# Moving the token-layout load of x, its norm and the first evacuation three weight chunks later in a hybrid decoder trunk

## The chip, the cores and the metric

The kernel runs on 1 core of one Trainium2 chip. The metric is the device time of one launch in microseconds (us), taken as the median of several runs.

## The reference, cut to what matters

One decoder layer on 256 tokens with 2048 features, all in f32. What the change touches is the very first step: the input is normalised by an RMS norm and multiplied by one wide projection.

```python
def rms_norm(x, g):
    xf = x.astype(jnp.float32)
    y = xf * lax.rsqrt(jnp.mean(xf * xf, axis=-1, keepdims=True) + EPS)
    return (y * g.astype(jnp.float32)).astype(x.dtype)
...
        h = rms_norm(x, g_mix[i])
        z = h @ w_in[i]
        (sc_b, sc_c, sc_x, cf_a, cf_g, q, k, v, g_out, gk_lr,
         m_a, m_b, m_c) = jnp.split(z, split_points, axis=-1)
```

Three token mixers (short convolution, Conformer convolution, gated linear attention), a merge, a SwiGLU FFN, a per-layer-embedding step and a final norm follow.

## The kernel before

**Products.** Every large product keeps the activations stationary (feature by token, 128x128 blocks) and streams weights of up to 512 columns. f32 accuracy comes from splitting both sides into a high and a low part and adding three matmuls: high by high (L244), high by the weight's low part (L245), low by the weight's high part (L246), all in `products`. A weight is split by `split` (L109): ScalarE writes `whi` (L110), VectorE writes `wlo` (L111).

**Groups and chunks.** A `Group` is one block of output columns; its 2048 input features are taken in four chunks of four 128-row tiles. A chunk is 24 matmuls (4 tiles, 2 halves of the tokens, 3 products). Chunks are numbered through the whole plan: the group `k` 0 is chunks 0 to 3, `k` 1 is 4 to 7, `gk` is 8 to 11, then `q`, `v` and so on.

**The loop.** `run` (L250) goes through the chunks. In iteration i it issues the transfers of chunk i+2 (`issue`, on the SP queue), splits chunk i+1 (`split_w`), runs what has been put off to this iteration (`deferred`), scales the activations that chunk i needs (`g.pre`, for the first group only), writes the matmuls, and after a group's last chunk calls its `evac`. This fixes the order in the source. The order on each engine's instruction stream can differ from it, which the rows of the engines' timelines show.

**The start.** The RMS norm is not applied to the input ahead of the first product. Its gain is: `h_pre` (L351) scales x by features (tiles `x`, 512 KB a chunk, transferred at L164 and L173) by `g_mix` and splits it into `hhi` (ScalarE, L321) and `hlo` (VectorE, L322 through the helper at L104). The root of the mean square is a factor per token, so it is applied when a group leaves PSUM. For that factor x is loaded a second time, by tokens: two tiles `xt` of 128x2048 (1024 KB each, L176). `x_norm` (L359) squares each on ScalarE with a running sum (L363) and makes the reciprocal root `rt` from the sums (a ScalarE square root at L301 and small VectorE operations).

**Where these steps stand.** `xt` is issued after the weights of chunks 3 and 4. `x_norm` is called by `ev_k0`, the evacuation of chunk 3. `ev_k0` puts the rest off to iteration 5: `load_consts` (SP transfers of `gnb` and two `lm` mask tiles, VectorE casts) and the evacuation proper, which copies the two accumulators, scaled by `rt`, into `fk` (ScalarE, L407) and puts their transposes off by two more iterations.

**Buffers.** `raws` and `wparts` have 5 buffers each, and a chunk takes two of them. The PSUM pool `acc` has 5 banks, and a group takes two. `xt` takes two of the 13 large tiles.

Of the kernel before, what the change touches and what calls it, by code (L numbers as in the profile page):

```python
# [28 lines left out]
LAG = 2  # L29
# [34 lines left out]
def kernel(  # L64
# [5 lines left out]
    nc = tc.nc  # L70
# [13 lines left out]
    def nm(s):  # L84
        uid[0] += 1
        return f"{s}_{uid[0]}"

    def big(name, shape=(P, 8, T), dt=F32):
        return t8.tile(list(shape), dt, tag="t8", name=nm(name))

    def med(name, shape=(P, 2, NB), dt=F32):
        return t4.tile(list(shape), dt, tag="t4", name=nm(name))
# [4 lines left out]
    def sm(name, n, tag):  # L97
        return small.tile([P, n], F32, tag=tag, name=nm(name))
# [50 lines left out]
    x_v = x[0].rearrange("(h p) d -> p h d", p=P)  # L149
# [3 lines left out]
    chunks = []  # L153
    state = {"dma": 0, "split": 0}

    def issue(c):
        g = c.g
        c.raw = []
        for k in c.ks[::2]:
            r = raws.tile([P, 2, g.n], F32, tag="raw", name=nm("raw"))  # L160
            if c is chunks[0]:

                for q in range(2):
                    nc.sync.dma_start(out=xs[0][:, k + q, :], in_=x_feat[:, k + q, :])  # L164
                    nc.sync.dma_start(out=r[:, q, :], in_=g.w[:, k + q, g.c0 : g.c0 + g.n])
            else:
                nc.sync.dma_start(out=r, in_=g.w[:, k : k + 2, g.c0 : g.c0 + g.n])
            c.raw.append(r)
        if c in chunks[:3]:
            z = chunks.index(c) + 1  # L170
            if z == 2:
                nc.sync.dma_start(out=vec[:, 16:], in_=vecs[:, 16:])
            nc.sync.dma_start(out=xs[z], in_=x_feat[:, 4 * z : 4 * z + 4, :])  # L173
        if c in chunks[3:5]:
            xt = big("xt", (P, D))
            nc.sync.dma_start(out=xt, in_=x_v[:, chunks.index(c) - 3, :])  # L176
            x_tok.append(xt)

    def split_w(c):
# [17 lines left out]
    deferred = []  # L197
# [3 lines left out]
    def defer(i, fn):  # L201
        deferred.append((i + LAG, fn))
# [47 lines left out]
    def run(plan):  # L250
# [3 lines left out]
        while now[0] < len(chunks):  # L254
            i = now[0]
            c = chunks[i]
            while state["dma"] < min(len(chunks), i + PREF_DMA + 1):
                issue(chunks[state["dma"]])
                state["dma"] += 1
# [37 lines left out]
    def rsqrt(ss, n, scale, tag):  # L297
        v = sm("v", n, tag + "v")
        ts(v, ss, scale, EPS, ALU.mult, ALU.add)
        s = sm("s", n, tag + "s")  # L300
        act.activation(out=s, in_=v, func=AF.Sqrt)  # L301
        y = sm("y", n, tag + "y")
        dve.reciprocal(out=y, in_=s)
        newton(y, s, v)
        return y
# [53 lines left out]
    def x_norm():  # L359

        ss = sm("sx", 2, "sx")
        for h in range(2):
            act.activation(out=x_tok[h], in_=x_tok[h], func=AF.Square, accum_out=ss[:, h : h + 1])  # L363
        rt["1"] = rsqrt(ss, 2, 1.0 / D, "rt")
        rt["q"] = sm("rq", 2, "rq")
        dve.tensor_scalar_mul(rt["q"], rt["1"], 0.0625)

    def rs(h, key="1"):
        return rt[key][:, h : h + 1]

    def load_consts():
        nc.sync.dma_start(out=gnb, in_=g_gla_norm[0].partition_broadcast(P))
        for a in range(0, 2 * NL + 1, 8):
            n = min(8, 2 * NL + 1 - a)
            lm = med("lm", (P, 8, P), I32)
            nc.sync.dma_start(out=lm[:, :n, :], in_=masks[:, a : a + n, :])
            dve.tensor_copy(lmask[:, a : a + n, :], lm[:, :n, :])
        nc.gpsimd.memset(cmask, 1.0)
        nc.gpsimd.memset(cmask.rearrange("p (c t) -> p c t", t=64)[:, :, 0:1], 0.0)
        nc.gpsimd.memset(sT, 0.0)  # L380
        dve.tensor_copy(flip, ident[:, ::-1])


    def to_feat(key, c, src):

        if c == 0:
            featT[key] = big(key + "T")

        def sink(j, b):
            act.activation(out=featT[key][:, 4 * c + j : 4 * c + j + 2, :], in_=b, func=AF.Copy)  # L390

        transpose_block(src, sink)

    def ev_k0(g, i):
        x_norm()

        def later():
            load_consts()
            ev_feat("k", 0)(g, i)

        defer(i, later)

    def ev_feat(key, c, rkey="1", then=None):
        def f(g, i):
            m = med("f" + key)
            for h in range(2):
                act.activation(out=m[:, h, :], in_=g.ps[h], func=AF.Copy, scale=rs(h, rkey))  # L407

            def later():
                to_feat(key, c, m)  # L410
                if c == 1 and then is not None:
                    then()

            defer(i, later)

        return f
# [369 lines left out]
    def Z(name, c, ev, n=NB, pre=None, kind="tok", off=0, cost=1.3):  # L786
# [4 lines left out]

    plan = [
        Z("k", 0, ev_k0, pre=h_pre),
        Z("k", 1, ev_feat("k", 1)),
        Z("gk", 0, ev_first, 264),
# [260 lines left out]
```

## Time and profile before

| | us |
|---|---|
| median of 3 runs | 1912.35 |
| lowest, highest | 1912.32, 1913.01 |
| profiled execution | 1912.33 |
| its span in the profile | 1910.6 |

The span is the time from the first to the last instruction that the profiler recorded; 1.73 us of the profiled execution lie outside it. Busy times of different engines overlap. A matmul's end is modelled, so its start times are what to compare. In a timeline row the first number is the start, the second the duration, and the brackets at the end, where there are any, hold the idle time of that engine just before and what ended it. SPq is the queue of SyncE that issues transfers; its duration is that of issuing, not of moving the data.

### The profile page before, as it was taken

Reading aid. Unit: us, or ns where it says so; the run is one execution under the profiler, and the core shown is the slowest. Engines: PE = TensorE matmul, PEld = TensorE weight load, DVE = VectorE, ACT = ScalarE, POOL = GpSimd, SP = SyncE. Lnnn points to the kernel's source line nnn. Section 1 sums busy time; section 2 is a strip of 40 time slices with the busy share of each in tenths; the row PEclk is TensorE's granted clock in tenths of the full one; section 3 lists DMA queues with packets and bytes.
Section 4 is the critical chain, followed back from the end, with each engine's and each line's share of the span. In section 5 each row is a group of like instructions: output and inputs, shape, how many; then the busy total and the mean of one; then the engine's idle time right before and its main releaser. Section 6 shows DMA issues by size and latency. Waiting matters only on the chain.

```text
span 1910.6 us, 22740 instructions
## 1 busy us (share of the span) xinstructions
PE 1887.1 (99%) x8688; PEld 1573.0 (82%) x8688; DVE 1188.8 (62%) x1409; ACT 927.3 (49%) x1067; POOL 9.1 (0%) x22
## 2 busy tenths in 40 slices
PE   7999999999999999999999999999999999999998
PEld 5888888888888888888888888888888888888887
DVE  6447777668888888655555555555555555555555
ACT  6557556554454435644445544444344444444554
POOL 0000000000000000000000000000000000000000
PEclk9999999999999999999999999999999999999999
DMA  8666655555666656676655666665566666655553
GB/s 306 204 187 187 177 177 179 174 165 166 189 186 194 193 165 209 195 232 193 213 187 184 185 191 192 189 189 190 195 192 192 195 188 189 192 186 191 180 186 122
DMA packets 190254, 363.18 MB, mean 190 GB/s; under 512 B 11600, under 2 KB 20432, under 8 KB 189760
## 3 DMA queue, kind: packets, MB, share of 16 engines
q1 hardware_dynamic: 189248, 358.12, 61.2%
q0 software_dynamic: 896, 3.61, 0.6%
q8 instruction: 68, 1.11, 0.2%
q14 instruction: 42, 0.34, 0.1%
HBM read 359.58 MB, written 2.10 MB: 189 GB/s over the span
## 4 chain that ended last, share of the span: by engine, by line
PE 98%; DMA 1%; DVE 1%; ACT 0%; SPq 0%; issue 0%; DVEq 0%
PE acc L244 32%; PE acc L246 32%; PE acc L245 31%; PE tr L313 2%; PE sc L522 1%; DMA xt<-in_x_dram 0%; DMA x<-in_x_feat_dram 0%; DVE rw L688 0%; DVE wlo L111 0%; PE ov L592 0%; PE ov L594 0%; PE ov L593 0%; ACT whi L110 0%; ACT hhi L321 0%; PE sc L549 0%
## 5 line engine op out<-in xcount | busy, mean ns | idle before, releaser
L111 DVE TENSOR_TENSOR wlo<-raw,whi 128x1024 fp32r<-128x1024 f32 (+2 forms) x678 | 813.7, 1203 | 678.0 <-ACT whi L110 677.1
L110 ACT ACTIVATE whi<-raw 128x1024 fp32r<-128x1024 f32 (+2 forms) x678 | 706.2, 1043 | 914.7 <-PE acc L246 836.5
L244 PE MATMUL acc<-whi,hhi 128*128 128x512 f32 (+1 forms) x1120 | 434.4, 388 | 12.1 <-ACT hhi L321 6.9
L245 PE MATMUL acc<-wlo,hhi 128*128 128x512 f32 (+1 forms) x1120 | 431.2, 385 | 0.4 <-DVE wlo L111 0.4
L246 PE MATMUL acc<-whi,hlo 128*128 128x512 f32 (+1 forms) x1120 | 431.3, 385 | 0.0
L244 PE MATMUL acc<-whi,xhi 128*128 128x512 f32 (+1 forms) x832 | 321.4, 386 | 0.0
L246 PE MATMUL acc<-whi,xlo 128*128 128x512 f32 (+1 forms) x832 | 320.5, 385 | 0.0
L245 PE MATMUL acc<-wlo,xhi 128*128 128x512 f32 (+1 forms) x832 | 320.2, 385 | 0.0
L244 PEld LDWEIGHTS acc<-whi,hhi 128*128 128x128 f32 x1120 | 211.5, 189 | 53.4 <-ACT hhi L321 7.3
L245 PEld LDWEIGHTS acc<-wlo,hhi 128*128 128x128 f32 x1120 | 211.7, 189 | 42.0 <-DVE wlo L111 1.2
L246 PEld LDWEIGHTS acc<-whi,hlo 128*128 128x128 f32 x1120 | 211.4, 189 | 42.0
L246 PEld LDWEIGHTS acc<-whi,xlo 128*128 128x128 f32 x832 | 156.3, 188 | 31.5
L245 PEld LDWEIGHTS acc<-wlo,xhi 128*128 128x128 f32 x832 | 156.4, 188 | 31.0
L244 PEld LDWEIGHTS acc<-whi,xhi 128*128 128x128 f32 x832 | 156.3, 188 | 30.7
L244 PE MATMUL acc<-whi,aT 128*128 128x512 f32 x352 | 137.5, 390 | 0.0
L246 PE MATMUL acc<-whi,aT 128*128 128x512 f32 x352 | 137.1, 389 | 0.0
L245 PE MATMUL acc<-wlo,aT 128*128 128x512 f32 x352 | 136.9, 389 | 0.0
L104 DVE SCALAR_TENSOR_TENSOR cv<-uT,vec,cv 128x255 f32<-128x255 f32 (+15 forms) x240 | 110.9, 467 | 4.8
L246 PEld LDWEIGHTS acc<-whi,aT 128*128 128x128 f32 x352 | 66.1, 188 | 13.9
L245 PEld LDWEIGHTS acc<-wlo,aT 128*128 128x128 f32 x352 | 66.1, 188 | 13.6
L244 PEld LDWEIGHTS acc<-whi,aT 128*128 128x128 f32 x352 | 66.1, 188 | 13.4
L244 PE MATMUL acc<-whi,mT 128*128 128x512 f32 x128 | 50.2, 392 | 0.0
(250 smaller groups left out, 1369.4 us busy)
## 6 DMA issues: line engine op xcount, KB each, us to landing
raw<-in_w_in_dram SPq DMA_DIRECT2D x262, 512.0 KB, 3.6
raw<-in_w_gate_up_dram SPq DMA_DIRECT2D x176, 512.0 KB, 3.7
raw<-in_w_down_dram SPq DMA_DIRECT2D x88, 512.0 KB, 3.6
raw<-in_w_gla_out_dram SPq DMA_DIRECT2D x32, 512.0 KB, 3.8
raw<-in_w_o_dram SPq DMA_DIRECT2D x32, 512.0 KB, 3.6
raw<-in_w_ple_gate_dram SPq DMA_DIRECT2D x24, 512.0 KB, 3.7
raw<-in_w_sc_out_dram SPq DMA_DIRECT2D x16, 512.0 KB, 4.2
raw<-in_w_cf_out_dram SPq DMA_DIRECT2D x16, 512.0 KB, 4.4
```

Of the source, the lines that this page charges most:

```text
L104: dve.scalar_tensor_tensor(out=o, in0=a, scalar=s, in1=b, op0=op0, op1=op1)
L110: a = act.activation(out=hi, in_=src, func=AF.Copy)
L111: b = dve.tensor_tensor(out=lo, in0=src, in1=hi.bitcast(F32), op=ALU.subtract)
L244: pe.matmul(o, lhsT=shi[:, hs], rhs=whi, start=st, stop=False)
L245: pe.matmul(o, lhsT=shi[:, hs], rhs=wlo, start=False, stop=False)
L246: pe.matmul(o, lhsT=slo[:, hs], rhs=whi, start=False, stop=sp)
L313: pe.transpose(b[:, q, h * P : h * P + P], src[:, h, (j + q) * P : (j + q) * P + P], ident,)
L522: pe.matmul(b[:, e, :], lhsT=K[:, dt, :], rhs=Q[:, dt, :], start=q == 0, stop=q == 1)
```

## The change

The two transfers of x by tokens are issued after the weights of chunks 5 and 6, not 3 and 4. `ev_k0` no longer calls `x_norm` at once: it puts off to iteration i + LAG + 1 = 6 the norm, the evacuation and then `load_consts`. The evacuation gets i + LAG + 1 as its iteration, so the transposes of its result go to iteration 8, not 6 (the code before put them off to 5, but in iteration 5, whose list had been taken already).

```diff
-        if c in chunks[3:5]:
+        if c in chunks[5:7]:
             xt = big("xt", (P, D))
-            nc.sync.dma_start(out=xt, in_=x_v[:, chunks.index(c) - 3, :])
+            nc.sync.dma_start(out=xt, in_=x_v[:, chunks.index(c) - 5, :])
             x_tok.append(xt)
...
     def ev_k0(g, i):
-        x_norm()
 
         def later():
+            x_norm()
+            ev_feat("k", 0)(g, i + LAG + 1)
             load_consts()
-            ev_feat("k", 0)(g, i)
-
-        defer(i, later)
+
+        deferred.append((i + LAG + 1, later))
```

## Rows read from the trace of the kernel before

**Rows 1.** The page's first lines: the span, and the busy time of the matmuls with its share of the span.

```profile
span 1910.6 us, 22740 instructions
PE 1887.1 (99%) x8688; PEld 1573.0 (82%) x8688; DVE 1188.8 (62%) x1409; ACT 927.3 (49%) x1067; POOL 9.1 (0%) x22
```

**Rows 2.** All waits of the matmuls over the whole run: who was waited for, us in total, times, longest.

```profile
PE acc L244 <- ACT hhi L321: 6.9, 1, 6.9
PE acc L244 <- ACT whi L110: 5.3, 1, 5.3
PE mu L690 <- DVE rw L688: 1.7, 1, 1.7
PE acc L245 <- DVE wlo L111: 0.4, 1, 0.4
```

**Rows 3.** The chain of work that ended last, 15 to 35 us: start, us, what.

```profile
15.15 9.32 DMA xt<-in_x_dram
24.49 1.40 ACT xt L363
...
26.49 0.41 ACT hhi L321
```

**Rows 4.** The timeline of ScalarE, 10 to 43 us. The `hhi` rows are of chunks 1, 2 and 3, the `whi` rows of chunks 1 (both halves in one row), 2, 2, 3, 3, 4, 4 in order of time.

```profile
10.79 1.71 ACT L321 ACTIVATE hhi<-x,vec 128x256 fp32r<-128x256 f32 x4 [1.39 <-DMA x<-in_x_feat_dram]
12.40 2.18 ACT L110 ACTIVATE whi<-raw 128x1024 fp32r<-128x1024 f32 x2
16.67 1.06 ACT L110 ACTIVATE whi<-raw 128x1024 fp32r<-128x1024 f32 x1 [2.08 <-DMA raw<-in_w_in_dram]
18.11 1.06 ACT L110 ACTIVATE whi<-raw 128x1024 fp32r<-128x1024 f32 x1 [0.38 <-DMA raw<-in_w_in_dram]
20.74 1.06 ACT L110 ACTIVATE whi<-raw 128x1024 fp32r<-128x1024 f32 x1 [1.57 <-DMA raw<-in_w_in_dram]
22.05 1.06 ACT L110 ACTIVATE whi<-raw 128x1024 fp32r<-128x1024 f32 x1 [0.25 <-DMA raw<-in_w_in_dram]
24.49 1.91 ACT L363 ACTIVATE xt<-xt 128x2048 f32<-128x2048 f32 x1 [1.38 <-DMA xt<-in_x_dram]
...
26.40 1.69 ACT L321 ACTIVATE hhi<-x,vec 128x256 fp32r<-128x256 f32 x4
28.00 1.04 ACT L110 ACTIVATE whi<-raw 128x1024 fp32r<-128x1024 f32 x1
28.94 1.69 ACT L321 ACTIVATE hhi<-x,vec 128x256 fp32r<-128x256 f32 x4
30.54 1.90 ACT L363 ACTIVATE xt<-xt 128x2048 f32<-128x2048 f32 x1
...
33.49 1.28 ACT L301 ACT_TABLE_LOAD   x1
...
41.33 1.25 ACT L407 ACTIVATE fk<-acc,y 128x512 f32<-128x512 f32 x2
```

**Rows 5.** The timeline of VectorE in the same stretch: the low parts of chunk 3's weights (two in one row), then those of chunk 2's activations.

```profile
21.83 2.54 DVE L111 TENSOR_TENSOR wlo<-raw,whi 128x1024 fp32r<-128x1024 f32 x2 [1.40 <-ACT whi L110]
26.92 1.69 DVE L104 SCALAR_TENSOR_TENSOR hlo<-x,vec,hhi 128x256 fp32r<-128x256 f32 x4 [2.56 <-ACT hhi L321]
```

**Rows 6.** The timeline of the matmuls: the last one of chunk 1, the first, eleventh and twelfth of chunk 2, and the first of chunk 3.

```profile
19.69 0.39 PE L246 MATMUL acc<-whi,hlo 128*128 128x512 f32 x1
26.94 0.79 PE L244 MATMUL acc<-whi,hhi 128*128 128x512 f32 x1 [6.86 <-ACT hhi L321]
...
31.38 0.52 PE L245 MATMUL acc<-wlo,hhi 128*128 128x512 f32 x1
31.73 0.39 PE L246 MATMUL acc<-whi,hlo 128*128 128x512 f32 x1
...
34.68 0.39 PE L244 MATMUL acc<-whi,hhi 128*128 128x512 f32 x1
```

**Rows 7.** Transfers. First the SP queue's timeline: the issue of the `x` tile of chunk 2 and of the first `xt`, then six weight transfers (chunks 5, 6 and 7) in one row and the first transfer of `load_consts`; then what all queues had moved from 0 to 20 us; then, of the same 20 us, the three 512 KB transfers of `x` (count, KB each, median us from issue to landing); last, the two `xt` transfers' time to landing.

```profile
7.28 0.66 SPq L173 DMA_DIRECT2D x<-in_x_feat_dram  x1
...
15.15 0.46 SPq L176 DMA_DIRECT2D xt<-in_x_dram  x1
...
20.45 17.19 SPq L167 DMA_DIRECT2D raw<-in_w_in_dram  x6
37.69 0.46 SPq L372 DMA_DIRECT2D gnb<-in_g_gla_norm_dram  x1
...
DMA packets 3359, 6.22 MB, mean 311 GB/s; under 512 B 414, under 2 KB 1054, under 8 KB 3359
...
x<-in_x_feat_dram SPq DMA_DIRECT2D x3, 512.0 KB, 8.0
...
DMA to landing us min/median/max: 9.3/9.8/10.3
```

**Rows 8.** Busy time by stretch: length, PE, PEld, DVE, ACT and POOL busy us (with the number of instructions), the granted TensorE clock (1.00 is 2.4 GHz, 0.50 is 1.2 GHz), the DMA engines' mean share and GB/s.

```profile
24.00:24.50 0.50, 0.00 (x0) 0.00 (x0) 0.36 (x1) 0.01 (x1) 0.00 (x0) 1.00 1.04 385
24.50:25.00 0.50, 0.00 (x0) 0.00 (x0) 0.00 (x0) 0.50 (x1) 0.00 (x0) 0.81 1.07 393
...
31.50:32.00 0.50, 0.50 (x4) 0.42 (x3) 0.38 (x1) 0.50 (x1) 0.06 (x1) 0.86 1.04 381
...
600.00:720.00 120.00, 120.00 (x531) 99.41 (x530) 105.43 (x173) 49.43 (x51) 0.00 (x0) 1.00 0.59 180
```

## The prediction

> **What bounds the kernel now.** I read the page first: the matmuls are busy for 1887.1 of 1910.6 us [rows 1], so only time in which TensorE waits, or runs at its lower clock, can be won. The list of its waits holds four, and one is long: 6.9 us, for `hhi` on ScalarE [rows 2]. The chain of waits shows what is behind it: for 9.32 us the transfer of the first `xt`, then the squaring, then `hhi`, then matmuls again [rows 3]. ScalarE's timeline shows why a squaring that nobody needs yet stops the products. The stream holds, in this order, both `whi` of chunk 3, the squaring of `xt`, the four `hhi` of chunk 2 [rows 4]. The squaring started at 24.49, when its transfer had landed, and `hhi` of chunk 2 behind it at 26.40. The input of that `hhi` was there long before: its transfer was issued at 7.28, and the three of that size took 8.0 us in the median, 10.0 for the longest if it was this one, so 15.3 to 17.3 us [rows 7]. So chunk 2 waits for a transfer that is not its own.
>
> What the wait costs is read from the matmuls [rows 6]. At full clock thirteen starts of chunk 2 take 34.68 - 31.73 = 2.95 us, 0.227 each. Chunk 1's last matmul started at 19.69, so chunk 2 could have started at 19.92 and started at 26.94: 7.02 us. Its first eleven starts took 31.73 - 26.94 = 4.79 us where 11 x 0.227 = 2.50 would do: 2.29 us more. The granted clock is 1.00 at 24.0 to 24.5 us, 0.81 in the next half and 0.86 at 31.5 to 32.0 [rows 8], so about from 24.8 to 31.6 it was at 1.2 GHz. The whole that can be won is 7.02 + 2.29 = 9.31 us.
>
> From 32 us on TensorE waited once more, 1.7 us for a sum of the Conformer norm [rows 2]. VectorE, which is late there, is busy for 105 of the 120 us from 600 to 720 [rows 8]; it is not full, and its weight splits follow the matmuls through the `wparts` buffers. So what is won at the start shifts all later work and comes off the end in full.
>
> **The change part by part.** *The squaring leaves its place.* Its transfer is now issued behind the weights of chunk 5. The second half of those takes the buffer that the first half of chunk 3 frees, when `wlo` is written: 21.83 + 2.54 / 2 = 23.1 us [rows 5]. A transfer of `xt` then lands 9.3 to 10.3 us later [rows 7], at 32.8 to 33.8, or sooner where less is queued. In the source the call now stands behind chunk 6's weight issue and split, three iterations later. I take it that the squaring then stands behind `hhi` of chunks 2 and 3: already before, the second `xt`, issued behind chunk 4's weights, stands behind both [rows 4].
>
> *What is late next.* The order of the rest I keep as it was: `whi`, `whi` of chunk 3, then `hhi` of chunk 2. Nothing that comes before these in a queue is changed, and before, `hhi` was placed behind both although its input had landed before chunk 2's weights. The second `whi` of chunk 3 runs from 22.05 to 23.11 [rows 4]. `hhi` then starts at 23.11, and the first matmul 26.94 - 26.40 = 0.54 us later: 23.65. The third needs `hlo`, and VectorE is on `wlo` of chunk 3 until 21.83 + 2.54 = 24.37; one `hlo` takes 1.69 / 4 = 0.42, so 24.79 [rows 5]. From there 22 starts of 0.227 = 4.99 lead to chunk 3's first matmul at 29.78. Before it was 34.68 [rows 6]: 4.90 us won.
>
> *Do chunk 3's weights land sooner?* By the sizes, what is queued up to them is 6.48 MB, and with `xt` 7.53 MB. By 20.0 us 6.22 MB had moved [rows 7]; at 390 GB/s, as later [rows 8], the rest takes until 20.7 and 23.4 us. They were seen at 22.05 and 24.49 [rows 4]: 1.4 and 1.1 us later. The `xt` behind came about as much later as its own size, so I take it that it did not hold them back and that 22.05 stays. The other end is that all of the 1.4 us goes: 6.3 us won. That they land later I exclude, since nothing new is put ahead of them.
>
> *The clock.* With the matmuls back at 23.65 and dense from 24.79, their wait falls from 7.02 to 3.7 us, with a second of 0.9 between. Before, the clock fell at about 24.8, after some 5 us without a matmul. No row shows what it does after less than that. The ends are 0 and the 2.29 us of before. I take 0, because at 24.0 to 24.5 the row still has 1.00, and by then the matmuls run again. The Trainium skill (TensorE: Matmul & The Clock Gate, Part 1) says that the low clock is the default state and that activity releases it; by that rule two matmuls in a long gap may not be enough to hold it, and the sum would be 2.61 us won, not 4.90. The trace agrees with it for the wait of 7.02 us, and none here shows a shorter one.
>
> *The norm and the evacuation.* The work is the same: two squarings of 1.9 us, a table load of 1.28, the root, small VectorE steps, and an evacuation of 1.25 [rows 4]. The second `xt` is issued behind chunk 6's weights, the last of which wait for the split of chunk 4's first half. That `whi` follows chunk 2's `hhi`, so this is at about 27 us; with 10.3 us it lands by 37.3. Squaring and table load end by 40.5. In the trace before, the root and what follows it reach the evacuation between 34.8 and 41.3, 6.5 us later [rows 4], though that includes waiting. The evacuation is then done by 48. The first that needs it is chunk 8, whose second accumulator is one of the two banks: at 29.78 + 5 x 24 x 0.227 = 57.0. The cover is 9 us of chunks 3 to 7. Without it each us late is a us of TensorE. On ScalarE the `whi` of chunks 5 and 6 queue behind the squarings; with the squarings ended at 39.2, chunk 5 starts at 40.7 and its second half 2.7 us later, so this is the nearest thing to a new wait: at nothing, at worst 1 us.
>
> *The queues.* On SP the two `xt` go behind four more weight transfers each, so chunk 4's weights come 1.0 MB sooner, and `load_consts` goes behind chunk 8's weights instead of 7's [rows 7]. Its users come after the projection's first groups. The transposes move within TensorE's stream, same count. All this I cost at nothing; what chunk 4's sooner weights could do is a rival below.
>
> **Sum.** 1912.33 is the profiled execution, 1912.35 the median, so both sums agree: 1912.35 - 4.90 = 1907.45, say 1907.5.
>
> **The rivals.** *The clock falls all the same.* Same order, but with the low clock on chunk 2: 4.90 - 2.29 = 2.61 us won, 1909.7. For it: the fall came at 24.8, when only two matmuls would have run since 19.9.
>
> *`hhi` moves up.* ScalarE has idle gaps of 1.57 and 0.25 us ahead of chunk 3's `whi` [rows 4], and `hhi` fits the first. Then the wait goes whole: 9.31 us, 1903.0. Between the two `whi`, it starts at 21.8, `hlo` is written by 23.1 + 0.4 = 23.5, chunk 3 starts at 28.5: 6.2 us, 1906.2. For it: `hhi` of chunk 1 stands ahead of chunk 1's own `whi`. Against it: chunk 2's did not, with the same input ready.
>
> *Something else takes the place.* With chunk 4's weights a megabyte sooner, its first `whi` may go ahead of `hhi`. They land 0.52 MB, 1.3 us, behind 22.05, at 23.4; `hhi` starts 1.06 us after that, `wlo` of chunk 4 goes ahead of `hlo`, and the third matmul is at 26.1: 1.3 us less won, 1908.8, and 1911.1 with the low clock.
>
> *Slower: the squaring stays ahead of `hhi`.* Before, it stood there although its call comes after chunk 3's products and `hhi` of chunk 2 before chunk 2's. If it does so again, moving its transfer back makes the same wait longer. The point from which it decides is a landing after 24.49; with 29.7 (queued in order) to 33.8 the matmuls start 5.2 to 9.3 us later: 1917.6 to 1921.7. Against it: the transfer now stands behind four more weight transfers, and the second `xt` took a place behind.
>
> **How the numbers follow.** Forecast 30%, `hhi` moves up 28%, clock falls 17%, something else ahead 16%, squaring ahead 9%. The likeliest is 1907.5; its own range, from the terms above, is 1906.0 to 1909.7. The range for 8 in 10 goes from 1903.0, where all is won, to 1911.0, and leaves out the slower case. About 0.2%, 3.8 us, can be told from no change by a measurement of this kernel. Faster by that: forecast and moved up, and 6 of the clock's 17, where it is low for less long than before: 64%. Within: the other 11 and the 16: 27%. Slower: 9%.
>
> **What would show it.** ScalarE's stream after: no squaring ahead of the `hhi` of chunks 2 and 3. TensorE's wait ahead of chunk 2: two pieces, 3.7 and 0.9 us, ended by `hhi` and then by VectorE, and chunk 3's first matmul near 29.8. Second `whi` of chunk 3 still at 22.05. A clock of 1.00 between 24 and 32. `fk` before 48 and no wait of chunks 5, 6 or 8. The forecast is wrong if the order on ScalarE ahead of chunk 2 is another one, which is the one thing on which most of the range hangs.

## The result, and the profile after

The changed kernel takes 1903.09 us (median of 4 runs, 1902.64 to 1903.29) beside 1912.43 for the kernel before (four runs now): a ratio of 0.995, 95% interval 0.9933 to 0.9967. The profiled execution took 1903.29 us with a span of 1901.4, 9.2 us less than before [rows 1]. The forecast was 1907.5; the rival that `hhi` moves up gave 1903.0 for the whole wait with its clock. The time lies outside the forecast's own range of 1906.0 to 1909.7, and only just inside the range for 8 in 10, whose lower end of 1903.0 is that rival.

The list of TensorE's waits shows at once that the long one, for `hhi`, is gone (who was waited for, us in total, times, longest):

```profile
PE acc L244 <- ACT whi L110: 5.1, 1, 5.1
PE mu L690 <- DVE rw L688: 1.7, 1, 1.7
PE acc L245 <- DVE wlo L111: 0.5, 1, 0.5
```

Of the four waits before [rows 2] three stand: the one for `whi`, which is ahead of the very first matmul, and two short ones. The one for `hhi` is missing altogether, where the forecast left 3.7 us of it. ScalarE's timeline shows why. The three rows of `hhi` are those of chunks 1, 2 and 3, and each of the first three `whi` rows is both halves of one chunk's weights. The single `whi` at 23.71 is the first half of chunk 4:

```profile
11.06 1.71 ACT L321 ACTIVATE hhi<-x,vec 128x256 fp32r<-128x256 f32 x4 [1.03 <-DMA x<-in_x_feat_dram]
12.68 2.16 ACT L110 ACTIVATE whi<-raw 128x1024 fp32r<-128x1024 f32 x2
15.58 1.71 ACT L321 ACTIVATE hhi<-x,vec 128x256 fp32r<-128x256 f32 x4 [0.74 <-DMA x<-in_x_feat_dram]
17.20 2.23 ACT L110 ACTIVATE whi<-raw 128x1024 fp32r<-128x1024 f32 x2
19.57 1.71 ACT L321 ACTIVATE hhi<-x,vec 128x256 fp32r<-128x256 f32 x4
21.19 2.24 ACT L110 ACTIVATE whi<-raw 128x1024 fp32r<-128x1024 f32 x2
23.71 1.06 ACT L110 ACTIVATE whi<-raw 128x1024 fp32r<-128x1024 f32 x1 [0.28 <-DMA raw<-in_w_in_dram]
...
31.35 1.92 ACT L363 ACTIVATE xt<-xt 128x2048 f32<-128x2048 f32 x1 [1.77 <-DMA xt<-in_x_dram]
...
36.42 1.92 ACT L363 ACTIVATE xt<-xt 128x2048 f32<-128x2048 f32 x1 [1.16 <-DMA xt<-in_x_dram]
...
48.16 1.25 ACT L407 ACTIVATE fk<-acc,y 128x512 f32<-128x512 f32 x2
```

Beside [rows 4]: `hhi` of chunk 2 no longer stands behind chunk 3's weights and a squaring. It stands ahead of chunk 2's own weights and starts when its input lands, at 15.58. The matmuls follow without a gap, and the granted clock stays at 2.4 GHz where it had fallen [rows 6, 8]. First the timeline of the matmuls: the last of chunk 1, the first two of chunk 2 and the first of chunk 3; then the stretches of rows 8:

```profile
19.93 0.39 PE L246 MATMUL acc<-whi,hlo 128*128 128x512 f32 x1
20.16 0.61 PE L244 MATMUL acc<-whi,hhi 128*128 128x512 f32 x2
...
25.60 0.39 PE L244 MATMUL acc<-whi,hhi 128*128 128x512 f32 x1
```

```profile
24.00:24.50 0.50, 0.50 (x4) 0.40 (x3) 0.50 (x1) 0.50 (x1) 0.00 (x0) 1.00 0.99 365
24.50:25.00 0.50, 0.50 (x4) 0.42 (x3) 0.38 (x2) 0.27 (x1) 0.00 (x0) 1.00 1.20 242
```

Chunk 3 starts at 25.60 instead of 34.68: 9.08 us sooner, and 9.2 come off the span. So nothing later takes it back.

### The profile page after: what moved, and what is told of

The parts are those of the page before. It is cut to its first block, busy times and chain, and to the rows that moved or that the text cites. A ratio compares the mean times of both kernels' runs of the same rounds, so it can differ in the third digit from the quotient of the medians.

```text
span 1901.4 us, 22742 instructions
## 1 busy us (share of the span) xinstructions
PE 1884.7 (99%) x8688; PEld 1570.9 (83%) x8688; DVE 1187.9 (62%) x1409; ACT 927.1 (49%) x1067; POOL 9.1 (0%) x22
## 4 chain that ended last, share of the span: by engine, by line
PE 98%; DVE 1%; DMA 0%; ACT 0%; SPq 0%; issue 0%; DVEq 0%
PE acc L246 32%; PE acc L245 32%; PE acc L244 32%; PE tr L313 2%; PE sc L522 1%; DMA x<-in_x_feat_dram 0%; DVE rw L688 0%; DVE wlo L111 0%; PE ov L593 0%; PE ov L594 0%; PE ov L592 0%; ACT whi L110 0%; PE sc L549 0%; SPq L165 0%; SPq L164 0%; ACT hhi L321 0%
```

## The experiments

Three theories were on trial. **Order:** what counts is where chunk 2's `hhi` stands in ScalarE's stream, and moving the load matters only because it changes that. **Transfer:** the 2 MB of x by tokens hold up the first weights. **Call:** the later place of the norm in the source is what helps. The times of the kernel before that stand beside each run are of the same chip: 1911.96 for runs 1 to 4, 1912.23 for 5 to 8, 1912.38 for 9 to 11.

**1. The later call alone**

```diff
 def ev_k0(g, i):
-        x_norm()
         def later():
+            x_norm()
+            ev_feat("k", 0)(g, i + LAG + 1)
             load_consts()
...
+        deferred.append((i + LAG + 1, later))
```

> Only the second part of the change: norm, evacuation and constants three chunks later, x by tokens still loaded with chunks 3 and 4. On ScalarE the first squaring still stands ahead of chunk 2's hhi. Order theory (what counts is where chunk 2's hhi stands on ScalarE): no change, 1912.4, with the wait of 6.9 us at 20 to 27 us as before. Call theory (the place of the norm in the source counts): 1903. Transfer theory (the 2 MB of x by tokens hold up the first weights): no change, 1912.4.

1911.89 us, ratio 1.0 (0.9991 to 1.001). ScalarE's timeline is that of before, with the squaring ahead of chunk 2's `hhi`, although its call now stands in iteration 6, four behind that `hhi`:

```profile
22.26 1.06 ACT L110 ACTIVATE whi<-raw 128x1024 fp32r<-128x1024 f32 x1 [0.25 <-DMA raw<-in_w_in_dram]
24.68 1.91 ACT L363 ACTIVATE xt<-xt 128x2048 f32<-128x2048 f32 x1 [1.37 <-DMA xt<-in_x_dram]
...
26.59 1.69 ACT L321 ACTIVATE hhi<-x,vec 128x256 fp32r<-128x256 f32 x4
```

The call theory falls: a later call does not move the squaring back in the stream.

**2. The later load, with the norm in iteration 5, where the evacuation stood before**

```diff
         def later():
             x_norm()
-            ev_feat("k", 0)(g, i + LAG + 1)
             load_consts()
+            ev_feat("k", 0)(g, i)
-        deferred.append((i + LAG + 1, later))
+        defer(i, later)
```

> The load with chunks 5 and 6 as in the change; norm and evacuation together in iteration 5, where the evacuation stood before, not 6. On ScalarE chunk 2's hhi stands ahead of chunk 2's own whi, as after the change. Order theory: 1903.1, as after the change, within 0.3. Transfer theory: 1903.1. Call theory (three chunks later is needed): slower than the change by a wait for the norm, 1905 or more.

The diff is against the kernel after. 1904.03 us, ratio 0.9957 (0.9942 to 0.9972), and no wait for `hhi`. The median is 0.9 us off the expected 1903.1, but its four runs go from 1903.0 to 1904.8, and one iteration more or less of the norm does nothing that the intervals tell apart. The load is not quite alone here: the norm's call stands in iteration 5, not 3, since it has to come behind the second transfer, which is issued in iteration 4. Run 1 has the later call without the load and wins nothing, so the load is the part that works.

**3. The load one chunk later, all else as before**

```diff
-        if c in chunks[3:5]:
+        if c in chunks[4:6]:
```

> The kernel before with x by tokens loaded with chunks 4 and 5, one chunk later; the norm is called where it was. On ScalarE chunk 2's hhi stands behind both whi of chunk 3 and ahead of both squarings, the order that my forecast assumed. Order theory: the forecast's sum, 1907.5 if the clock holds through a wait of 3.7 us and one of 0.9, 1909.8 if it falls. Transfer theory: x by tokens is out of the way of chunk 3's weights, so near the whole gain, 1903 to 1905. Call theory: 1912.4.

1909.03 us, ratio 0.9986 (0.9976 to 0.9995): 2.9 us won of the 9.3. This is the forecast's own order on ScalarE, so its working can be read line by line. In turn the wait, ScalarE from chunk 3's `whi`, VectorE, the matmuls of chunk 2 (first and third) with the first of chunk 3, and the granted clock by stretch:

```profile
PE acc L244 <- ACT hhi L321: 3.6, 1, 3.6
```

```profile
20.96 1.06 ACT L110 ACTIVATE whi<-raw 128x1024 fp32r<-128x1024 f32 x1 [1.58 <-DMA raw<-in_w_in_dram]
22.30 1.06 ACT L110 ACTIVATE whi<-raw 128x1024 fp32r<-128x1024 f32 x1 [0.29 <-DMA raw<-in_w_in_dram]
23.27 1.69 ACT L321 ACTIVATE hhi<-x,vec 128x256 fp32r<-128x256 f32 x4
```

```profile
22.05 2.57 DVE L111 TENSOR_TENSOR wlo<-raw,whi 128x1024 fp32r<-128x1024 f32 x2 [1.41 <-ACT whi L110]
24.54 1.67 DVE L104 SCALAR_TENSOR_TENSOR hlo<-x,vec,hhi 128x256 fp32r<-128x256 f32 x4
```

```profile
23.81 0.79 PE L244 MATMUL acc<-whi,hhi 128*128 128x512 f32 x1 [3.56 <-ACT hhi L321]
...
25.07 0.80 PE L246 MATMUL acc<-whi,hlo 128*128 128x512 f32 x1
...
32.10 0.39 PE L244 MATMUL acc<-whi,hhi 128*128 128x512 f32 x1
```

```profile
22.00:22.50 0.50, 0.00 (x0) 0.00 (x0) 0.45 (x1) 0.21 (x2) 0.00 (x0) 0.80 1.05 385
22.50:23.00 0.50, 0.00 (x0) 0.00 (x0) 0.50 (x1) 0.50 (x1) 0.00 (x0) 0.50 1.05 389
...
29.00:29.50 0.50, 0.50 (x3) 0.38 (x2) 0.00 (x0) 0.43 (x2) 0.24 (x1) 0.87 0.98 397
```

The forecast had the first matmul at 23.65 and the third at 24.79; they start at 23.81 and 25.07, behind `hhi` and then behind `hlo`, as worked out. But the clock fell at about 22.3 us, before the matmuls were back, and chunk 3 starts at 32.10, not 29.78. From the third matmul to chunk 3 the 22 starts take 32.10 - 25.07 = 7.03 us where the forecast had 4.99, so by this count the low clock cost 2.04 us here. The sum with the low clock said 2.61 us won; 34.68 - 32.10 = 2.58. That they agree so well is partly luck: the third matmul starts 0.28 us later than forecast, and the clock costs 0.25 less than the 2.29 of that sum.

**4. The order alone: the squarings tied behind chunk 3's `hhi`, the transfers where they were**

```diff
-        act.activation(out=hi, in_=src, func=AF.Copy, scale=s)
+        rt["hhi"] = act.activation(out=hi, in_=src, func=AF.Copy, scale=s).ins
...
-            act.activation(out=x_tok[h], in_=x_tok[h], func=AF.Square, ...)
+            with tc.issue_after(rt["hhi"]):
+                act.activation(out=x_tok[h], in_=x_tok[h], func=AF.Square, ...)
```

> The kernel before, transfers and calls where they were; the two squarings are only tied behind the last hhi of chunk 3 on ScalarE. Chunk 2's hhi stands behind both whi of chunk 3, as in the run with the load one chunk later. Order theory: the same time as that run, 1907.5 or 1909.8 by the clock. Transfer theory and call theory: 1912.4, since neither was moved; by the transfer theory chunk 3's weights also land later here than in that run, by 1.3 us or more.

`issue_after` puts what stands under it behind the named instruction on that engine. 1909.47 us, ratio 0.9985 (0.9975 to 0.9994): not to be told from run 3, though no transfer was moved. ScalarE, the same three steps; then the third matmul of chunk 2, the first of chunk 3, and the stretch in which the clock fell:

```profile
21.06 1.06 ACT L110 ACTIVATE whi<-raw 128x1024 fp32r<-128x1024 f32 x1 [1.58 <-DMA raw<-in_w_in_dram]
22.38 1.06 ACT L110 ACTIVATE whi<-raw 128x1024 fp32r<-128x1024 f32 x1 [0.26 <-DMA raw<-in_w_in_dram]
23.34 1.69 ACT L323 ACTIVATE hhi<-x,vec 128x256 fp32r<-128x256 f32 x4
```

```profile
25.14 0.80 PE L246 MATMUL acc<-whi,hlo 128*128 128x512 f32 x1
...
32.71 0.39 PE L244 MATMUL acc<-whi,hhi 128*128 128x512 f32 x1
```

```profile
23.50:24.00 0.50, 0.11 (x1) 0.12 (x1) 0.50 (x1) 0.50 (x2) 0.00 (x0) 0.55 1.01 385
```

Chunk 3's second half starts at 22.38 with a transfer of `xt` queued right behind it, and at 22.30 in run 3 without; the first half is 0.10 later too. So `xt` does not hold those weights back, as the forecast took it. The clock fell at about 23.55 here, with the same wait of 3.6 us, and the 22 starts take 32.71 - 25.14 = 7.57 us: the low clock cost 2.58.

**5. The order of the kernel after, with the load and the call of the kernel before**

```diff
 def split_w(c):
+        if c.g.pre is h_pre and c is not chunks[0]:
+            c.g.pre(c.ks)
...
+                    with tc.issue_after(rt["hhi"]):
+                        c.ins = split(hi, lo, r)
```

> The kernel before, with x by tokens still loaded with chunks 3 and 4 and the norm called where it was; on ScalarE each chunk's hhi is tied ahead of its own whi and the squarings behind the last hhi, the order of the kernel after. Order theory: the whole gain, 1903.1, with no wait of TensorE ahead of chunk 2. Transfer theory: the 2 MB still stand ahead of chunk 4's weights, so part of the gain is missing, 1905 or more. Call theory: 1912.4.

The ties of run 4 are kept. 1903.04 us, ratio 0.9953 (0.9938 to 0.9968): the whole gain, with no wait of TensorE for `hhi`. ScalarE starts chunk 2's `hhi` as the input lands, and a squaring stands ahead of a later `whi` without harm:

```profile
15.41 1.71 ACT L329 ACTIVATE hhi<-x,vec 128x256 fp32r<-128x256 f32 x4 [0.72 <-DMA x<-in_x_feat_dram]
17.02 2.23 ACT L110 ACTIVATE whi<-raw 128x1024 fp32r<-128x1024 f32 x2
...
27.02 1.90 ACT L370 ACTIVATE xt<-xt 128x2048 f32<-128x2048 f32 x1
```

The transfer theory falls: with the 2 MB where they were, nothing of the gain is missing.

**6. The wait of the kernel before, filled with matmuls**

```diff
...
                 products(g, c, (0, 1))
+                if i == 1:
...
+                    with tc.issue_after(last_mm[0]):
+                        for _ in range(28):
+                            pe.matmul(fill, lhsT=ones, rhs=fw, start=True, stop=True)
```

> The kernel before with 28 extra matmuls of 512 columns on data that is there (their result is not used), placed in TensorE's wait ahead of chunk 2; nothing else is changed, and the wait ends when it did. It prices the clock alone. If the low clock on chunk 2 is the price of the idle time: the first eleven starts of chunk 2 go from 4.79 to 2.5 us and the time falls by 2.3, to 1910.1. If it falls for another reason, or the gain is all the wait: 1912.4.

1910.31 us, ratio 0.999 (0.9981 to 1.0), and 1908.6 us of span where the kernel before has 1910.6. The interval ends at 1.0, so the time alone hardly shows the gain; the starts of the matmuls do. The filling, the first of chunk 2 and its twelfth:

```profile
20.11 6.58 PE L291 MATMUL fill<-hhi,ones 128*128 128x512 f32 x28
27.15 0.50 PE L244 MATMUL acc<-whi,hhi 128*128 128x512 f32 x1 [0.46 <-ACT hhi L328]
...
29.83 0.39 PE L246 MATMUL acc<-whi,hlo 128*128 128x512 f32 x1
```

The first eleven starts take 29.83 - 27.15 = 2.68 us instead of 4.79 [rows 6], though chunk 2's `hhi` comes as late as ever. So the low clock was worth 2.1 us of the 9.3, and the wait the rest.

**7. Later still: load with chunks 7 and 8, norm in iteration 7**

```diff
-        if c in chunks[5:7]:
+        if c in chunks[7:9]:
...
-            ev_feat("k", 0)(g, i + LAG + 1)
+            ev_feat("k", 0)(g, i + LAG + 2)
...
-        deferred.append((i + LAG + 1, later))
+        deferred.append((i + LAG + 2, later))
```

> The change taken further: x by tokens with chunks 7 and 8, norm and evacuation in iteration 7. The cover of the norm is tested. Its second bank is needed by chunk 8, in the kernel after at 53.6 us. If the norm runs as late as I work out (second squaring ends near 48, evacuation some 10 us later as in the kernel after), TensorE waits some 5 us ahead of chunk 8's second half: 1908, and with the low clock up to 1910. If the cover is as wide as my forecast said (9 us): 1903 to 1904.

The diff is against the kernel after. 1902.56 us, ratio 0.9949 (0.9935 to 0.9964): no wait, so the expectation of 1908 was a miss. ScalarE, the end of the second squaring and the evacuation; then VectorE, the first and the last small step ahead of the evacuation; then the first matmul of chunk 8:

```profile
47.03 0.18 ACT L363 ACTIVATION_READ_ACCUMULATOR xt<-xt 128x1 f32 x1
...
50.24 1.26 ACT L407 ACTIVATE fk<-acc,y 128x512 f32<-128x512 f32 x2 [0.98 <-DVE y L101]
```

```profile
47.24 0.17 DVE L107 TENSOR_SCALAR v<-sx 128x2 f32<-128x2 f32 x1 [1.18 <-ACT xt L363]
...
50.05 0.15 DVE L101 TENSOR_TENSOR y<-y,s 128x2 f32<-128x2 f32 x1
```

```profile
52.63 0.28 PE L244 MATMUL acc<-whi,hhi 128*128 128x264 f32 x1
```

The squaring ended about where I had put it, but the evacuation came 3 us behind it, not 10. In the kernel after the same small steps stand between weight splits:

```profile
38.45 0.17 DVE L107 TENSOR_SCALAR v<-sx 128x2 f32<-128x2 f32 x1 [1.75 <-ACT xt L363]
...
46.39 0.16 DVE L101 TENSOR_TENSOR y<-y,s 128x2 f32<-128x2 f32 x1
```

In run 7 one split stands between them, there four do, with waits of VectorE for `whi` between. So most of the ten microseconds there is waiting, and not the work of the norm. The evacuation of run 7 is done at 51.5, some 1 us before chunk 8 starts. Later than this was not tried.

**8 and 9. The squaring kept ahead of `hhi`, with the transfer one chunk later**

```diff
-        if c in chunks[3:5]:
+        if c in chunks[4:6]:
...
 def h_pre(ks):
+            if c == 2:
+                rt["ss"] = sm("sx", 2, "sx")
+                st.enter_context(tc.issue_after(square(0)))
```

> The slower rival, made on purpose: x by tokens loaded one chunk later, with chunks 4 and 5, and the first squaring tied ahead of chunk 2's hhi on ScalarE. By the rival's rule the matmuls start as much later as the transfer lands later than 24.49; behind 1 MB more of weights that is some 2.7 us: 1915 us, 1914 to 1916. If the squaring's place did not matter (transfer theory): 1909, as with the load one chunk later alone.

1910.31 us, ratio 0.9991 (0.9982 to 1.0). A miss of the time, with a reason in the program: half of chunk 4 had been put ahead of chunk 2 in TensorE's stream. Its twelve matmuls run from 24.68 and fill part of the wait. Chunk 2 starts at 29.78, which is 2.8 us later than before [rows 6], as expected:

```profile
24.68 1.22 PE L244 MATMUL acc<-whi,hhi 128*128 128x512 f32 x2 [4.53 <-ACT whi L110]
...
29.78 0.50 PE L244 MATMUL acc<-whi,hhi 128*128 128x512 f32 x1
```

So the run was made again with those matmuls tied behind chunk 3's (and chunk 3's `hhi` behind chunk 2's):

```diff
...
+                    if i == 4:
+                        st.enter_context(tc.issue_after(last_mm[0]))
                     products(g, c, (0, 1))
```

> The slower rival again, since in the run before TensorE filled its wait with half of chunk 4. The load with chunks 4 and 5, the first squaring tied ahead of chunk 2's hhi, chunk 3's hhi tied behind that, and chunk 4's matmuls tied behind chunk 3's. The transfer should land near 27.3 as in the run before, not at 24.49: TensorE starts chunk 2 some 2.8 us later than in the kernel before: 1915. If the place of the squaring costs nothing by itself: 1910 or less.

1914.65 us, ratio 1.0012 (1.0003 to 1.0021): slower than before. The wait, then ScalarE:

```profile
PE acc L244 <- ACT hhi L327: 9.6, 1, 9.6
```

```profile
27.37 1.91 ACT L370 ACTIVATE xt<-xt 128x2048 f32<-128x2048 f32 x1 [2.70 <-DMA xt<-in_x_dram]
...
29.28 3.29 ACT L327 ACTIVATE hhi<-x,vec 128x256 fp32r<-128x256 f32 x8
```

The transfer lands at 27.37 instead of 24.49, 2.9 us later, and the wait is 9.6 us instead of 6.9 [rows 2]. So the rule by which the slower rival was priced holds. A later load wins 9.3 us (the change) or 2.9 (run 3), or costs 2.3 (here), by the order on one engine.

**10 and 11. The kernel after and run 7 side by side, five rounds**

> The changed kernel beside the next run on one chip, to tell the two apart. Order theory: 1903.

> The load with chunks 7 and 8 and the norm in iteration 7 once more, beside the changed kernel. If the cover is all that counts, the same time as the changed kernel within 0.5 us; if moving the 2 MB away from the start wins more, 0.5 to 1 us less.

1902.22 and 1902.23 us, ratios 0.9949 (0.9935 to 0.9962) and 0.995 (0.9938 to 0.9963): no difference. Whether the load stands behind chunk 5 or two chunks further back does not matter once the squaring is out of the way.

## Why the prediction was wrong

**What bounds the start: right.** The wait of 7.02 us and the 2.29 of low clock behind it were the whole of what could be won there. All 9.31 were: 9.3 measured. Run 6 gives the clock's share as 2.1; the other 0.2 of the 2.29 is lost at full clock too, in the first three starts (27.15 to 28.01, where 3 x 0.227 = 0.68 would do). That nothing later takes the gain back held too; the span fell by what chunk 3 gained.

**The step that failed** is *what is late next*: "The order of the rest I keep as it was". It left 4.4 of the 9.31 us unwon; with the order that came, chunk 2 does not wait at all. `hhi` of chunk 2 was kept behind both `whi` of chunk 3, on the ground that nothing ahead of them in a queue is changed. Here the order on ScalarE did not depend on what stands ahead alone. Moving a transfer that comes later in the SP queue moved `hhi` past four `whi`: behind chunk 3's weights or chunk 4's the load leaves it late (runs 1 and 3), behind chunk 5's it comes early (run 2). Run 5 sets the same order by hand, with the load and the call where they were, and wins the same 9.2 us; so the order is the cause. Why the building of the program changes the order is not seen in a trace and stays open. The rival that `hhi` moves up was given 28% beside 30% for the forecast, with the argument for it in plain view: chunk 1's `hhi` already stood ahead of its own weights. The prediction named another order on ScalarE as the one sign that it was wrong, and that is what showed.

**The sum for the order that was assumed** is tested by runs 3 and 4, which have that order. The starts were right within 0.4 us, VectorE as the second wait among them. The term of the clock was not: I took 0, and it cost 2.04 us in run 3 and 2.58 in run 4. So even with its order the forecast of 1907.5 would have been some 2 us too low, and 1909.7, the rival with the low clock, was measured as 1909.0 and 1909.5. I had reasoned from one stretch of one run, that the clock still stood at 1.00 at 24.0 to 24.5 us [rows 8]. In run 3 it fell at 22.3, 2.4 us after the start of the last matmul. The Trainium skill (TensorE: Matmul & The Clock Gate, Part 1) calls the low clock the default state, which activity has to release. Run 3 agrees with that: when the matmuls came back at 23.81 the clock was at 0.50, and it rose again at about 29.1, with matmuls running since then.

That no row of before shows a shorter wait was a slip: the 1.7 us ahead of the matmul into `mu` [rows 2] are one, and the clock stays at 1.00 there. The stretch in the kernel before:

```profile
731.00:732.00 1.00, 0.00 (x0) 0.00 (x0) 1.00 (x1) 0.90 (x1) 0.00 (x0) 1.00 0.97 377
```

This would not have settled what a wait of 3.7 us costs.

**Chunk 3's weights and the transfers: right.** Their start moved by 0.08 us with `xt` behind them or not (runs 3 and 4). Chunk 4's weights, which the rival *something else takes the place* had land at 23.4, were split from 23.71, and no `hhi` stood behind them.

**The norm and its cover: right in effect.** The evacuation began at 48.16 and was done at 49.4, where it was to be done by 48, and nothing waited for it. The cover was about 4.5 us and not 9, since chunk 8 starts at 53.60 in the kernel after. One reading of the source was off, though the sum does not use it: in iteration 6 the call stands behind the issue of chunk 8 and the split of chunk 7, not chunk 6's.

**The slower rival** did not come about, but its rule holds: with the squaring tied ahead, a landing 2.9 us later makes the first matmul of chunk 2 start 2.9 us later (29.82 in run 9) and the run 2.3 us slower. The landings of 29.7 to 33.8 for which it was priced were not tried.

## What to carry to other kernels

When an engine that is not the bound holds up the one that is, find the instruction at the head of its stream and ask what that one waits for: here a squaring whose result the evacuation used 17 us later [rows 4]. Before trusting that a change of a transfer keeps the rest of an order, consider both orders and price each: here a transfer that comes later changed the order ahead of it. An explicit tie between instructions gave the same gain with the transfer left where it was (run 5). Price a wait of TensorE with the low clock behind it, even where one run shows the clock still up.

## What was not expected of the hardware

The clock falls at very different times after the last matmul: at about 24.8 us in the kernel before, 22.3 in run 3 and 23.55 in run 4, each with the last matmul started at 19.7 to 20.0. A wait of 3.6 us cost 2.0 to 2.6 us of low clock, and the one of 6.9 us cost 2.3 by the same count. No run shows what decides when it falls.
